# Two score banks held as one lasting tile, and each pair's score products as one chain, in a two-block transformer kernel

## The chip, the cores and the metric

The kernel runs on one core of one Trainium2 chip. The time is that of one execution on the device, in microseconds; the median of three runs stands for the kernel.

The engines of the core work side by side, each through its own queue in order: PE multiplies matrices (its weight loads are shown as PEld), DVE and ACT do vector and activation work, POOL some more vector work, SP starts most transfers. PE writes its products into PSUM, which has banks of 512 float32 columns; DVE and ACT read them from there.

## The reference, cut to what matters

A whole model in float32. The first block has four branches (an attention with forget gates, a gated linear recurrence, a stick-breaking attention, an attention to a memory), a gated merge and a feed-forward part. The second block has two layers, on 256 tokens and 256 context tokens, and in the second layer only the tokens go on. Each layer has three branches, a merge, and 16 experts that choose their tokens:

```python
ka, va, kb, vb, qa, qb, u, v, gates = _split(h @ w_in[i], KV_SIZES + Q_SIZES)
...
ya = neighbourhood_attn(_na_heads(qa), _na_heads(ka), _na_heads(va),
                        _na_heads(kac), _na_heads(vac), na_rpb[i])
kb_all = jnp.concatenate([_da_qk(kbc), rope_2d(_da_qk(kb), tabs)], axis=1)
yb = diff_head_norm(diff_attn_blocks(rope_2d(_da_qk(qb), tabs), kb_all, vb_all, lam),
                    da_subln_g[i], lam_init)
yc = gmlp_gate(jax.nn.gelu(u), jax.nn.gelu(v), gm_ln_g[i], gm_ln_b[i], gm_w_s[i], gm_b_s[i])
x = x + gt1 * branch_merge(ya, yb, yc, gates, w_branch[i], w_out[i])
...
x = x + gt2 * ec_moe(h2, w_router[i], w_e1[i], w_e3[i], w_e2[i])
```

The neighbourhood attention has 8 heads of 64 and adds a bias by position to part of its scores. The differential attention has 4 heads, each with two score matrices of depth 64: it takes the softmax of both and subtracts the second, times a factor lambda, from the first.

## The kernel before, in words

The weights are far too many to stay on the chip. They come from HBM in pieces of 1 MB, started by SP into a ring of buffers. ACT writes the rounded high part of each piece (`wh`, line 88), DVE the remainder (`wl`, line 91), and PE multiplies high by high, low by high and high by low, so that three products stand for one in float32. Operands in the activations are split the same way (`lph`/`lpl`, `hh`/`hl`). These products carry the name `mm` in the trace and are called weight products below. In the expert stage of the second block (`w_e` in the trace) the stream of weights is densest.

Attention is woven into them: `weave` takes so many steps of the weight products of one stage, then one step of an attention that is ready. Layer by layer the neighbourhood attention (`na_attn`) stands beside the projections of the differential attention, and the differential attention (`da_attn`) beside the first merge and the projections of the third branch. An attention's step is a turn of `pipe`, which has three units under way: the output products of unit i-2 (`pv`), the transposes of unit i-1 (`tp`, called turns below; the method is `turn`), and the scores of unit i (`s<-g`). A unit is 128 queries of two heads (neighbourhood) or of one head with its two score matrices (differential). `before` splits the q and k of the next unit into high and low, on ACT and POOL.

The two score matrices of a unit are a pair: `pair()` (line 360) asks a pool for two PSUM buffers with the tag "s", of which the pool has two, and `mm3_pair` (line 364) writes three products into each. As a head is 64 deep, such a product uses 64 of the 128 rows of PE's array, one score matrix the upper 64, the other the lower. Then for each matrix `softmax` follows: the maximum on DVE (line 344, `nm<-s`), the exponential on ACT, which also sums (`g<-s,nm`), the reciprocal on DVE (line 348, `r<-su`). In layer 0 half of the units have 512 columns of scores, half 256; in layer 1 all have 512. That makes 48 units, 32 of 512 columns and 16 of 256.

The same two buffers serve other work, one at a time: the rotary embedding of the differential attention's q and k (`rope`, line 1299, `s<-lb,cst` or `s<-lc,cst` in the trace), the memory attention, the recurrence, the mixing of the third branch, and in the expert stage the router, the gathering of tokens and the scattering of the results (`scatter`, `s<-g,ys`).

The order of the instructions on each engine isn't written out. A scheduler takes the traced program, keeps what depends on what (buffers of a pool included: a tile with the tag "s" may be written when the reader of the tile two before it is done), and sets the order of each engine by priority and by when it expects things to be ready. On the chip each engine then runs its queue in order: an instruction that waits holds up all behind it on its engine.

Of the kernel before, what the change touches and what calls it, by code (L numbers as in the profile page):

```python
# [9 lines left out]
F32 = mybir.dt.float32  # L10
# [65 lines left out]
class K:  # L76
# [276 lines left out]
    def gsplit(self, x):  # L353
# [4 lines left out]
        return h, l  # L358

    def pair(self):  # L360

        return [self.ps.tile([128, 512], F32, tag="s", name="s", bufs=2) for _ in range(2)]

    def mm3_pair(self, outs, abs_):

        for x, y, start, stop in ((0, 0, True, False), (0, 1, False, False), (1, 0, False, True)):
            for out, (a, b) in zip(outs, abs_):
                self.mm(out, a[x], b[y], start, stop)

# [5 lines left out]
    def run(self):  # L375
        nc, tc, a = self.nc, self.tc, self.a
        with ExitStack() as st:
            def pool(name, bufs, **k):
                return st.enter_context(tc.tile_pool(name=name, bufs=bufs, **k))

            self.glob = pool("glob", 1)
            self.small = pool("small", 1)
            self.ring = pool("ring", 3)
            self.ps = pool("ps", 1, space=PSUM)
            self.count = 0
            self.bc = None
            self.sqp = None
            self.pend = []
            self.setup()
            self.fill = self.mods()  # L390
            self.consts = [{}, {}]
            self.every, self.nmod = PLAN["every"], 0
            self.block1()
            self.lper = st.enter_context(tc.tile_pool(name="lper", bufs=1, side="right", reuse_waits="tile"))
            self.hh2, self.hl2 = self.lp("h", [128, KD, 512], F32R), self.lp("l", [128, KD, 512], F32R)
            self.block1_ffn()
            self.every = 0
            for i in range(2):
                self.layer(i)
            self.final()  # L400
# [254 lines left out]
    def fox_attn(self):  # L655
# [5 lines left out]
        def scores(hp):  # L661
            Ps = []

            ss = self.pair()
            for j, s in enumerate(ss):
                r = slice(64 * j, 64 * j + 64)
                self.mm(s[:, 0:128], q[r, hp, 0:128], k[r, hp, 0:128], True, False)
            for j, s in enumerate(ss):
                r = slice(64 * j, 64 * j + 64)
                self.mm(s[:, 128:384], q[r, hp, 128:256], k[r, hp], False, False)  # L670
            for j, s in enumerate(ss):
# [47 lines left out]
    def sb_attn(self):  # L719
# [4 lines left out]
        def weights(hp):  # L724
            Ps = []
            ss = self.pair()
            for j, s in enumerate(ss):
                r = slice(64 * j, 64 * j + 64)
                self.mm(s[:, 0:128], q[r, hp, 0:128], k[r, hp, 0:128], True, False)
            for j, s in enumerate(ss):  # L730
                r = slice(64 * j, 64 * j + 64)
                self.mm(s[:, 128:384], q[r, hp, 128:256], k[r, hp], False, False)
            for s in ss:
# [61 lines left out]
    def lru(self):  # L795
        nc, a = self.nc, self.a
# [29 lines left out]
        for k in range(KD):  # L826
            ps = self.ps.tile([128, 512], F32, tag="s", name="s", bufs=2)
            self.mm(ps[:, 0:256], bd["lru_w_a"][:, k], xc[:, k])
            self.mm(ps[:, 256:512], bd["lru_w_x"][:, k], xc[:, k])
            r = self.gtile()  # L830
# [78 lines left out]
    def mem_attn(self):  # L909
# [5 lines left out]
        def scores(u):  # L915
            h, qb = u
            qs = slice(qb * 128, qb * 128 + 128)
            s = self.ps.tile([128, 512], F32, tag="s", name="s", bufs=2)
            for k in range(2):
                self.mm(s[:, 0:256], mq[:, 2 * h + k, qs], mk[:, 2 * h + k], k == 0, k == 1)  # L920
            P = self.gtile(256)
            self.softmax(s, 256, P)
            return P
# [373 lines left out]
    def rope(self, x):  # L1297
        for m in range(4):
            ps = self.ps.tile([128, 512], F32, tag="s", name="s", bufs=2)[:, :256]
            xm = x[:, m, 0:256]  # L1300
# [95 lines left out]
    def gm_gate(self):  # L1396
# [19 lines left out]
        for t in range(nt):  # L1416
# [3 lines left out]
            self.tt(v, v, lb, ALU.add)  # L1420
            ps = self.ps.tile([128, 512], F32, tag="s", name="s", bufs=2)
            for g in range(4):
# [42 lines left out]
    def moe_pre(self, i):  # L1465
# [26 lines left out]
        self.xs = [self.X, self.XC][:ns]  # L1492
        self.lg = self.ps.tile([128, 512], F32, tag="s", name="s", bufs=2)

# [9 lines left out]
    def moe(self, i, st):  # L1504
# [18 lines left out]
        with tc.tile_pool(name=f"mh{i}", bufs=1, reuse_waits="tile") as hp:  # L1523
# [43 lines left out]
            for t in range(nt):  # L1567
                for kq in range(2):
                    tp = self.ps.tile([128, 512], F32, tag="s", name="s", bufs=2)
                    for k in range(4):  # L1570
# [23 lines left out]
        for e in range(NE):  # L1594
            if e % 4 == 0:
# [7 lines left out]
                for k in range(KD):  # L1603
                    ps = self.ps.tile([128, 512], F32, tag="s", name="s", bufs=2)[:, :ns * 128]
                    for m in range(ns):
# [71 lines left out]
    def scatter(self, i, pi, ys, slot2, aff2, sel, T, xs, gt2):  # L1677
        nc, tmp = self.nc, self.tmp
        sp = self.ps.tile([128, 512], F32, tag="s", name="s", bufs=2)[:, :T]
        self.mm(sp, sel[:, pi], slot2)  # L1680
        ap = self.ps.tile([128, 512], F32, tag="s", name="s", bufs=2)[:, :T]
        self.mm(ap, sel[:, pi], aff2)
# [6 lines left out]
        for ms in ([0], [1]) if ns == 2 and pi == NE // 2 - 1 else [range(ns)]:  # L1689
            if ms == [1]:  # L1690
                self.bc = self.rms_bc([xs[0]], idle=True)
            for d in range(KD):
                ps = self.ps.tile([128, 512], F32, tag="s", name="s", bufs=2)
                t = slice(256 * ms[0], 256 * ms[-1] + 256)
# [110 lines left out]
```

## Time and profile before

| | us |
|---|---|
| runs of the kernel before | 2762.38 median of 3 (2761.77 to 2765.89) |
| the profiled execution | 2762.17 |
| its span, from first to last instruction | 2760.4 |
| PE busy in the span | 2533.3 (92%) |
| DVE busy | 1256.9 (46%) |
| ACT busy | 885.1 (32%) |
| POOL busy | 153.2 (6%) |

The chain of work that ended last puts 81% of the span on PE, 13% on DMA, 4% on DVE and 1% on ACT. The mean granted clock of PE is 0.962 of full speed. Between the span and the execution's time lie 1.8 us.

The busy shares are means over stages that are limited by different things. In a timeline a row is a run of like instructions one after the other on an engine, with the start of the first, the time to the end of the last, and their number; the ends of PE's products are modelled, so neighbouring runs may overlap by a few hundredths of a microsecond. The operands in the shapes of PE's rows are the size of the weights (rows x columns) and the moving operand.

### The profile page before, as it was taken

Reading aid. Unit: us, or ns where it says so; the run is one execution under the profiler, and the core shown is the slowest. Engines: PE = TensorE matmul, PEld = TensorE weight load, DVE = VectorE, ACT = ScalarE, POOL = GpSimd, SP = SyncE. Lnnn points to the kernel's source line nnn. Section 1 sums busy time; section 2 is a strip of 40 time slices with the busy share of each in tenths; the row PEclk is TensorE's granted clock in tenths of the full one; section 3 lists DMA queues with packets and bytes.
Section 4 is the critical chain, followed back from the end, with each engine's and each line's share of the span. In section 5 each row is a group of like instructions: output and inputs, shape, how many; then the busy total and the mean of one; then the engine's idle time right before and its main releaser. Section 6 shows DMA issues by size and latency. Waiting matters only on the chain.

```text
span 2760.4 us, 41216 instructions
## 1 busy us (share of the span) xinstructions
PE 2533.3 (92%) x16928; PEld 1818.5 (66%) x16928; DVE 1256.9 (46%) x2550; ACT 885.1 (32%) x1672; POOL 153.2 (6%) x240
## 2 busy tenths in 40 slices
PE   8999999989999999999999999998999987767676
PEld 8999989979988777788843333335888882212222
DVE  6766675658742556664431221214357761101101
ACT  5754445446442334433220100103334441101011
POOL 1000110000001121100000000001221000000000
PEclk9999999999999999999999999999999998988887
DMA  7454645576674222132799999997443588999997
GB/s 232 156 184 153 199 149 181 174 231 210 201 231 118 68 52 77 53 102 92 264 373 409 409 409 409 409 408 235 102 65 124 185 311 356 409 409 409 409 409 279
DMA packets 361052, 666.15 MB, mean 241 GB/s; under 512 B 14256, under 2 KB 260272, under 8 KB 360864
## 3 DMA queue, kind: packets, MB, share of 16 engines
q1 hardware_dynamic: 354816, 654.15, 65.0%
q0 software_dynamic: 2896, 7.80, 2.4%
q8 instruction: 133, 2.18, 0.3%
q10 hardware_dynamic: 3152, 1.57, 0.2%
q14 instruction: 55, 0.45, 0.0%
HBM read 662.43 MB, written 1.05 MB: 240 GB/s over the span
## 4 chain that ended last, share of the span: by engine, by line
PE 81%; DMA 13%; DVE 4%; ACT 1%; issue 1%; SPq 0%; DVEq 0%; ACTq 0%
PE mm L103 67%; DMA w<-in_w_e 10%; PE s L103 9%; PE pv L103 3%; PE tp L372 3%; DMA lph<-in_w_e 1%; DVE g L100 1%; DMA w<-in_w_ada 1%; DVE X L100 1%; ACT g L88 0%; DMA w<-in_w_in 0%; DVE lpl L100 0%; DVE hT L1661 0%; ACT lph L88 0%; DVE wl L91 0%
## 5 line engine op out<-in xcount | busy, mean ns | idle before, releaser
L91 DVE TENSOR_TENSOR wl<-w,wh 128x1024 fp32r<-128x1024 f32 (+1 forms) x381 | 464.1, 1220 | 387.4 <-ACT wh L88 380.8
L88 ACT ACTIVATE wh<-w 128x1024 fp32r<-128x1024 f32 (+1 forms) x381 | 401.3, 1055 | 565.6 <-PE mm L103 487.5
L103 PE MATMUL mm<-w,xin 128*32 128x512 f32 (+1 forms) x1808 | 389.9, 649 | 68.9 <-DMA w<-in_w_e 67.4
L103 PEld LDWEIGHTS mm<-w,xin 128*32 128x32 f32 (+1 forms) x1808 | 96.2, 126 | 313.0 <-issue 173.4
L100 DVE SCALAR_TENSOR_TENSOR g<-g,mm 128x512 f32<-128x512 f32 (+1 forms) x64 | 43.9, 686 | 566.2 <-ACT g L88 510.6
L103 PE MATMUL mm<-lph,wh 128*128 128x512 f32 (+1 forms) x704 | 251.8, 358 | 2.4 <-DVE la L100 1.3
L103 PE MATMUL mm<-lph,wl 128*128 128x512 f32 (+1 forms) x704 | 248.0, 356 | 0.5 <-DVE wl L91 0.5
L103 PE MATMUL mm<-w,hT 128*32 128x256 f32 (+1 forms) x1320 | 171.7, 531 | 24.9 <-DVE hT L1661 11.2
L88 ACT ACTIVATE g<-mm 128x256 f32<-128x256 f32 (+2 forms) x126 | 57.4, 464 | 377.6 <-PE mm L103 336.3
L88 ACT ACTIVATE ys<-mm 32x256 f32<-32x256 f32 (+1 forms) x96 | 42.9, 447 | 388.7 <-PE mm L103 387.7
L103 PE MATMUL mm<-hh,wh 128*128 128x256 f32 x520 | 150.3, 289 | 2.6 <-ACT wh L88 2.6
L103 PEld LDWEIGHTS mm<-lph,wh 128*128 128x128 f32 x704 | 135.0, 192 | 24.3 <-issue 3.7
L372 PE MATMUL tp<-cst,g 128*128 128x128 f32 (+1 forms) x642 | 105.3, 277 | 48.5 <-DVE g L100 45.6
L103 PEld LDWEIGHTS mm<-lph,wl 128*128 128x128 f32 x704 | 134.4, 191 | 22.8 <-issue 4.5
L103 PE MATMUL mm<-hh,wl 128*128 128x256 f32 x520 | 148.7, 286 | 0.0
L103 PE MATMUL mm<-hl,wh 128*128 128x256 f32 x520 | 148.5, 286 | 0.0
L103 PEld LDWEIGHTS mm<-w,hT 128*32 128x32 f32 (+1 forms) x1320 | 67.2, 139 | 115.4 <-issue 77.6
L103 PE MATMUL mm<-lpl,wh 128*128 128x512 f32 x352 | 140.6, 399 | 0.0
L372 PEld LDWEIGHTS tp<-cst,g 128*128 128x128 f32 (+1 forms) x642 | 72.1, 142 | 97.2 <-issue 44.8
L103 PE MATMUL mm<-la,wh 128*128 128x512 f32 (+1 forms) x512 | 129.2, 340 | 0.1
L103 PE MATMUL mm<-a,wh 128*128 128x256 f32 x640 | 119.3, 286 | 0.0
L100 DVE SCALAR_TENSOR_TENSOR X<-s,mod,X 128x256 f32<-128x256 f32 x96 | 45.4, 483 | 155.2 <-PE s L103 155.2
(354 smaller groups left out, 5276.2 us busy)
## 6 DMA issues: line engine op xcount, KB each, us to landing
w<-in_w_e SPq DMA_DIRECT2D x335, 1024.0 KB, 18.4
w<-in_w_in SPq DMA_DIRECT2D x108, 1024.0 KB, 5.2
lph<-in_w_e SPq DMA_DIRECT2D x49, 1024.0 KB, 18.3
w<-in_w_ada SPq DMA_DIRECT2D x48, 1024.0 KB, 5.4
w<-in_w_up SPq DMA_DIRECT2D x22, 1024.0 KB, 5.2
w<-in_w_branch SPq DMA_DIRECT2D x16, 1024.0 KB, 5.1
w<-in_w_out SPq DMA_DIRECT2D x12, 1024.0 KB, 5.2
w<-in_w_branch SPq DMA_DIRECT2D x24, 512.0 KB, 3.4
```

Source lines behind the costliest of these rows:

```text
L88: return self.nc.scalar.activation(out, in_, func, **k)
L91: return (eng or self.nc.vector).tensor_tensor(out=out, in0=a, in1=b, op=op)
L100: return (eng or self.nc.vector).scalar_tensor_tensor(out=out, in0=a, scalar=s, in1=b, op0=op0, op1=op1)
L103: return self.nc.tensor.matmul(out, lhsT, rhs, start=start, stop=stop)
L372: self.nc.tensor.transpose(out, in_, self.ident[:n, :n])
```

## The change

The pool's two buffers "s" become one PSUM tile of 1024 columns that lasts for the whole program, `s2`, seen as two banks. `pair()` returns both. `sbank()` hands out one of the two, strictly in turn as the program is traced, to all other uses. Since the tile lasts, what may be written when follows from who last read or wrote that bank.

A pair's products run as a chain: in `together()` each product is traced with high priority, and each but the first is held, in PE's order, right behind the one traced before it. The bank that the softmax reads last (bank 1) gets its products first. The order of the three terms changes too: high by low and low by high come first, high by high last, so the first product needs the low part of k, which POOL makes. Operands and results stay the same.

The core of the diff (seven more places replace the pool's tile by `sbank()` as in the last piece; the pair of the stick-breaking attention changes as that of the forget-gate attention does):

```diff
@@ -357,15 +357,40 @@
         self.split(h, l, x, self.nc.gpsimd)
         return h, l
 
+    def sbank(self):
+
+        self.sn ^= 1
+        return self.s2[self.sn]
+
     def pair(self):
 
-        return [self.ps.tile([128, 512], F32, tag="s", name="s", bufs=2) for _ in range(2)]
+        return self.s2
+
+    @contextmanager
+    def together(self):
+
+        mm, last = self.mm, []
+
+        def chained(*a):
+            with self.tc.high_priority():
+                ins = mm(*a)
+            if last:
+                self.tc.keep_in_program_order(ins)
+            last.append(ins)
+            return ins
+
+        self.mm = chained
+        yield
+        del self.mm
 
     def mm3_pair(self, outs, abs_):
 
-        for x, y, start, stop in ((0, 0, True, False), (0, 1, False, False), (1, 0, False, True)):
-            for out, (a, b) in zip(outs, abs_):
-                self.mm(out, a[x], b[y], start, stop)
+
+
+        with self.together():
+            for x, y, start, stop in ((0, 1, True, False), (1, 0, False, False), (0, 0, False, True)):
+                for out, (a, b) in list(zip(outs, abs_))[::-1]:
+                    self.mm(out, a[x], b[y], start, stop)
 
     def transpose(self, out, in_):
         n = in_.shape[0]
@@ -382,6 +407,8 @@
             self.small = pool("small", 1)
             self.ring = pool("ring", 3)
             self.ps = pool("ps", 1, space=PSUM)
+            s2 = self.ps.tile([128, 1024], F32, name="s")
+            self.s2, self.sn = (s2[:, 0:512], s2[:, 512:1024]), 0
             self.count = 0
             self.bc = None
             self.sqp = None
@@ -662,12 +689,13 @@
             Ps = []
 
             ss = self.pair()
-            for j, s in enumerate(ss):
-                r = slice(64 * j, 64 * j + 64)
-                self.mm(s[:, 0:128], q[r, hp, 0:128], k[r, hp, 0:128], True, False)
-            for j, s in enumerate(ss):
-                r = slice(64 * j, 64 * j + 64)
-                self.mm(s[:, 128:384], q[r, hp, 128:256], k[r, hp], False, False)
+            with self.together():
+                for j in (1, 0):
+                    r = slice(64 * j, 64 * j + 64)
+                    self.mm(ss[j][:, 0:128], q[r, hp, 0:128], k[r, hp, 0:128], True, False)
+                for j in (1, 0):
+                    r = slice(64 * j, 64 * j + 64)
+                    self.mm(ss[j][:, 128:384], q[r, hp, 128:256], k[r, hp], False, False)
             for j, s in enumerate(ss):
                 h = 2 * hp + j
                 fh = self.fsel[:, h:h + 1]
...
     def rope(self, x):
         for m in range(4):
-            ps = self.ps.tile([128, 512], F32, tag="s", name="s", bufs=2)[:, :256]
+            ps = self.sbank()[:, :256]
             xm = x[:, m, 0:256]
             self.mm(ps, self.perm, xm)
```

PE's queue around a unit of layer 1's differential attention, before (`mm<-` with `wh`, `wl` or `lph` are weight products, `s<-g` the scores):

```order
L103 MATMUL mm<-wh,lph 128x256
L103 MATMUL s<-g 128x512 x3
L103 MATMUL mm<-wh,lhl 128x256
L103 MATMUL mm<-wl,lph 128x256
L103 MATMUL mm<-wh,lph 128x256
L103 MATMUL s<-g 128x512 x3
L103 MATMUL mm<-wh,lhl 128x256
```

and after:

```order
L103 MATMUL mm<-wl,lph 128x256
L103 MATMUL mm<-lph,wh 128x256
L103 MATMUL s<-g 128x512 x6
L397 MATMUL tp<-cst,g 128x128 x4
L103 MATMUL mm<-lhl,wh 128x256
L103 MATMUL mm<-lph,wl 128x256
```

The two runs of three, one bank each, with three weight products between them, have become one run of six. All 48 units stand so after the change; before, 9 stood as a run of six.

PE's queue at the end of layer 1's differential attention, before (`pv` are output products; the last row is the first weight product of what follows):

```order
L103 MATMUL mm<-lph,wl 128x256
L103 MATMUL s<-g 128x512 x3
L372 MATMUL tp<-cst,g 128x128 x4
L103 MATMUL pv<-lb_18434,g 128x128 x2
L103 MATMUL pv<-lb_18435,g 128x128 x2
L372 MATMUL tp<-cst,g 128x128 x4
L103 MATMUL pv<-lb_18434,g 128x128 x2
L103 MATMUL pv<-lb_18435,g 128x128 x2
L103 MATMUL mm<-lph,wh 128x256
```

and after:

```order
L103 MATMUL mm<-lph,wl 128x256
L103 MATMUL s<-g 128x512 x6
L397 MATMUL tp<-cst,g 128x128 x4
L103 MATMUL pv<-lb_18164,g 128x128 x2
L103 MATMUL pv<-lb_18165,g 128x128 x2
L397 MATMUL tp<-cst,g 128x128 x4
L103 MATMUL s<-g 128x512 x6
L103 MATMUL pv<-lb_18164,g 128x128 x2
L103 MATMUL pv<-lb_18165,g 128x128 x2
L103 MATMUL s<-g 128x512 x6
L397 MATMUL tp<-cst,g 128x128 x4
L103 MATMUL pv<-lb_18164,g 128x128 x2
```

Before, half a pair and then the turns and outputs of two units stand there without weight products. Now three whole pairs do, and the last rows of the piece go on with another output, a turn and two outputs before the weight products return.

PE's queue at the end of layer 0's neighbourhood attention, before (`s<-lb,cst` is a product of the rotary embedding, `s<-g 128x512` at the end the first differential unit):

```order
L103 MATMUL pv<-g,la_10301 64x128 x7
L372 MATMUL tp<-cst,g 128x128 x2
L103 MATMUL s<-g 128x256 x3
L372 MATMUL tp<-cst,g 128x128 x2
L103 MATMUL s<-g 128x256 x3
L103 MATMUL pv<-g,la_10301 64x128 x4
L372 MATMUL tp<-cst,g 128x128 x4
L103 MATMUL pv<-g,la_10301 64x128 x4
L103 MATMUL s<-g 128x512 x2
```

and after, from the first turn behind the last six weight products:

```order
L397 MATMUL tp<-cst,g 128x128 x4
L103 MATMUL s<-lb_10874,cst 128x256
L103 MATMUL pv<-g,la_10254 64x128
L397 MATMUL tp<-cst,g 128x128 x4
L103 MATMUL s<-g 128x512 x6
L103 MATMUL pv<-g,la_10254 64x128 x7
L397 MATMUL tp<-cst,g 128x128 x4
L103 MATMUL s<-lb_10874,cst 128x256
L103 MATMUL pv<-g,la_10254 64x128
L397 MATMUL tp<-cst,g 128x128 x4
L103 MATMUL s<-g 128x256 x6
L103 MATMUL pv<-g,la_10254 64x128 x7
```

Two units of 512 columns and two of 256 now come after the weight products have thinned out (the second of 256 is a few rows further down), where two of 256 came before.

DVE's queue for a unit at the end of layer 1's differential attention, before (`nm<-s` is the maximum, `r<-su` the reciprocal of the sum, `g<-tp` the copy of the transposed scores, `o<-pv` that of the output):

```order
L344 TENSOR_REDUCE nm<-s 128x1
L100 SCALAR_TENSOR_TENSOR g<-g,r 128x512
L344 TENSOR_REDUCE nm<-s 128x1
L91 TENSOR_TENSOR wl<-w,wh 128x1024
L701 COPY g<-tp 128x512
L348 RECIPROCAL r<-su 128x1 x2
L91 TENSOR_TENSOR r<-r,lamv_15012 128x1
L96 TENSOR_SCALAR g<-g,r 128x512
L100 SCALAR_TENSOR_TENSOR g<-g,r 128x512
```

and after:

```order
L344 TENSOR_REDUCE nm<-s 128x1
L729 COPY g<-tp 128x512
L348 RECIPROCAL r<-su 128x1
L344 TENSOR_REDUCE nm<-s 128x1
L348 RECIPROCAL r<-su 128x1
L91 TENSOR_TENSOR r<-r,lamv_14872 128x1
L96 TENSOR_SCALAR g<-g,r 128x512
L1386 COPY o<-pv 128x128
L100 SCALAR_TENSOR_TENSOR g<-g,r 128x512
```

The two maxima came ahead of both reciprocals; now the first bank's reciprocal stands between them, and no `wl` of a weight piece does.

## Rows read from the trace of the kernel before

**Rows 1.** Windows: from, to, length; busy per engine (instructions); clock, DMA share, GB/s.

```profile
860.00:1030.00 170.00, 170.00 (x1015) 133.24 (x1013) 82.30 (x163) 57.01 (x110) 27.61 (x31) 1.00 0.29 70
1030.00:1050.00 20.00, 19.05 (x116) 12.78 (x116) 11.44 (x30) 5.82 (x16) 3.48 (x4) 1.00 0.01 1
...
1137.00:1157.00 20.00, 14.56 (x75) 11.49 (x75) 12.13 (x40) 7.95 (x28) 2.86 (x4) 0.66 0.11 38
...
1385.00:1910.00 525.00, 494.29 (x2334) 192.81 (x2330) 126.99 (x297) 66.04 (x129) 3.78 (x5) 1.00 1.00 391
...
2080.00:2100.00 20.00, 20.00 (x155) 17.64 (x154) 14.18 (x24) 8.82 (x16) 2.60 (x3) 1.00 0.42 128
2100.00:2144.00 44.00, 44.00 (x334) 39.13 (x333) 32.26 (x61) 23.11 (x51) 7.98 (x6) 1.00 0.49 167
2144.00:2160.00 16.00, 11.30 (x66) 9.37 (x65) 13.06 (x35) 6.84 (x19) 2.46 (x4) 0.89 0.60 206
2260.00:2760.00 500.00, 347.03 (x2409) 123.17 (x2408) 62.45 (x150) 55.84 (x131) 0.78 (x2) 0.85 0.96 382
```

**Rows 2.** Groups by shape, layer 0's attentions: count, busy us, mean ns, idle before.

```profile
L103 PE MATMUL s<-g 64*128 64x512 f32 x96 | 23.7, 448 | 0.0
...
L103 PE MATMUL s<-g 64*128 64x256 f32 x96 | 17.1, 347 | 0.0
```

**Rows 3.** The same, layer 1's attentions.

```profile
L103 PE MATMUL s<-g 64*128 64x512 f32 x96 | 25.7, 441 | 0.0
```

**Rows 4.** Timeline of PE, a unit of layer 1: start, us, instruction, count.

```profile
1983.91 0.96 PE L103 MATMUL s<-g 64*128 64x512 f32 x6
```

**Rows 5.** Timeline of PE, another unit of layer 1.

```profile
2047.37 0.97 PE L103 MATMUL s<-g 64*128 64x512 f32 x3
```

**Rows 6.** Timeline of PE, a unit of 256 columns in layer 0.

```profile
929.95 0.62 PE L103 MATMUL s<-g 64*128 64x256 f32 x6
```

**Rows 7.** Timeline of PE, a pair of the forget-gate attention.

```profile
177.23 0.93 PE L103 MATMUL s<-a,a 64*128 64x128 f32 x8
```

**Rows 8.** Timeline of all engines, the end of layer 1's differential attention.

```profile
2146.95 0.96 PE L103 MATMUL s<-g 64*128 64x512 f32 x3
...
2147.95 0.69 DVE L344 TENSOR_REDUCE nm<-s 128x1 f32<-128x512 f32 x1 [0.56 <-PE s L103]
...
2148.74 0.69 ACT L88 ACTIVATE g<-s,nm 128x512 f32<-128x512 f32 x1
2149.33 0.19 ACT L88 ACTIVATION_READ_ACCUMULATOR g<-s,nm 128x1 f32 x1
...
2150.30 0.21 DVE L348 RECIPROCAL r<-su 128x1 f32<-128x1 f32 x2
...
2150.81 0.49 DVE L96 TENSOR_SCALAR g<-g,r 128x512 f32<-128x512 f32 x1
2151.33 0.75 DVE L100 SCALAR_TENSOR_TENSOR g<-g,r 128x512 f32<-128x512 f32 x1
...
2152.23 0.63 PE L372 MATMUL tp<-cst,g 128*128 128x128 f32 x4 [0.64 <-DVE g L100]
...
2152.97 0.69 DVE L701 COPY g<-tp 128x512 f32<-128x512 f32 x1 [0.68 <-PE tp L372]
...
2153.71 1.16 PE L103 MATMUL pv<-lb,g 128*128 128x128 f32 x8 [0.85 <-DVE g L701]
...
2156.15 0.47 PE L103 MATMUL mm<-lph,wh 128*128 128x256 f32 x1 [1.28 <-DVE la L100]
```

**Rows 9.** Timeline of PE, expert stage of layer 0, two units of scattering.

```profile
1474.98 1.98 PE L103 MATMUL s<-g,ys 128*128 128x512 f32 x4
1476.89 2.79 PE L103 MATMUL mm<-w,xin 128*64 128x512 f32 x10
```

**Rows 10.** The same stage, one unit of scattering.

```profile
1713.21 1.12 PE L103 MATMUL s<-g,ys 128*128 128x512 f32 x2
1714.27 1.93 PE L103 MATMUL mm<-w,xin 128*64 128x512 f32 x6
```

More of the change, by code (lines that the diff above doesn't have):

```diff
@@ L1 @@
 import math
-from contextlib import ExitStack
+from contextlib import ExitStack, contextmanager
 import numpy as np
@@ L726, in weights @@
             ss = self.pair()
[L727 to L732, printed above, removed]
+            with self.together():
+                for j in (1, 0):
+                    r = slice(64 * j, 64 * j + 64)
+                    self.mm(ss[j][:, 0:128], q[r, hp, 0:128], k[r, hp, 0:128], True, False)
+                for j in (1, 0):
+                    r = slice(64 * j, 64 * j + 64)
+                    self.mm(ss[j][:, 128:384], q[r, hp, 128:256], k[r, hp], False, False)
             for s in ss:
@@ L826, in lru @@
         for k in range(KD):
-            ps = self.ps.tile([128, 512], F32, tag="s", name="s", bufs=2)
+            ps = self.sbank()
             self.mm(ps[:, 0:256], bd["lru_w_a"][:, k], xc[:, k])
@@ L917, in scores @@
             qs = slice(qb * 128, qb * 128 + 128)
-            s = self.ps.tile([128, 512], F32, tag="s", name="s", bufs=2)
+            s = self.sbank()
             for k in range(2):
@@ L1420, in gm_gate @@
             self.tt(v, v, lb, ALU.add)
-            ps = self.ps.tile([128, 512], F32, tag="s", name="s", bufs=2)
+            ps = self.sbank()
             for g in range(4):
@@ L1492, in moe_pre @@
         self.xs = [self.X, self.XC][:ns]
-        self.lg = self.ps.tile([128, 512], F32, tag="s", name="s", bufs=2)
+        self.lg = self.sbank()
     def moe_front(self, k):
@@ L1568, in moe @@
                 for kq in range(2):
-                    tp = self.ps.tile([128, 512], F32, tag="s", name="s", bufs=2)
+                    tp = self.sbank()
                     for k in range(4):
@@ L1603, in moe @@
                 for k in range(KD):
-                    ps = self.ps.tile([128, 512], F32, tag="s", name="s", bufs=2)[:, :ns * 128]
+                    ps = self.sbank()[:, :ns * 128]
                     for m in range(ns):
@@ L1678, in scatter @@
         nc, tmp = self.nc, self.tmp
-        sp = self.ps.tile([128, 512], F32, tag="s", name="s", bufs=2)[:, :T]
+        sp = self.sbank()[:, :T]
         self.mm(sp, sel[:, pi], slot2)
-        ap = self.ps.tile([128, 512], F32, tag="s", name="s", bufs=2)[:, :T]
+        ap = self.sbank()[:, :T]
         self.mm(ap, sel[:, pi], aff2)
@@ L1692, in scatter @@
             for d in range(KD):
-                ps = self.ps.tile([128, 512], F32, tag="s", name="s", bufs=2)
+                ps = self.sbank()
                 t = slice(256 * ms[0], 256 * ms[-1] + 256)
```

## The prediction

> **What bounds the kernel now.** I read the stretches first, because the mean over the program (PE 92% busy) hides three kinds of stage. In the two attention parts of the second block PE has no gap: 170.00 us busy of 170 between 860 and 1030, 44.00 of 44 between 2100 and 2144, while DVE is busy 82.30 of the 170 us and ACT 57.01 [rows 1]. There a microsecond less on PE is a microsecond less of the span. The first layer's expert stage (1385 to 1910) has PE at 494.29 of 525 us, with its DMA share at 1.00 and the clock full: mostly PE. The second layer's (2260 to 2760) has PE at 347.03 of 500 us under a DMA share of 0.96: it waits for weights. Its transfers run back to back, but start only when the stage before it is done with the buffers, so what is won or lost ahead of it should shift it whole.
>
> Between the full stretches lie the ends of the two attentions, where the weight products beside which they are woven have run out. There PE does wait: 0.95 us of 20 at the end of layer 0's neighbourhood attention (1030 to 1050), 5.44 of 20 at the end of its differential attention (1137 to 1157, clock 0.66), nothing at the end of layer 1's neighbourhood attention (2080 to 2100), 4.70 of 16 at the end of its differential attention (2144 to 2160, clock 0.89) [rows 1]. I call these ends A, B, C and D.
>
> Then the groups of score products, for what they cost altogether, the timeline around single units, for what a pair costs when it runs together, and the timeline of end D, for the latency of one unit without cover.
>
> **The gain: the pairs.** The score products of these two attentions work with 64 rows of the array, so two of them can run side by side if they follow each other. Today they seldom do, since the two banks come free at different times and the scheduler puts weight products between. Altogether they take 23.7 us (512 columns) and 17.1 us (256 columns) in layer 0, and 25.7 us in layer 1 [rows 2, 3]: 66.5 us for 48 units of six products (288 in all). A run of six, both heads in turn, lasts 0.96 us [rows 4]; a run of three, one head alone, 0.97 us [rows 5]. So a whole pair costs what half of one does. With 256 columns a run of six lasts 0.62 us [rows 6]. In the changed order of PE all 48 units are such a run of six: 32 of 512 columns at 0.96 and 16 of 256 at 0.62, 30.7 + 9.9 = 40.6 us. PE gets 66.5 - 40.6 = 25.9 us back; I allow 2 either way, since the modelled ends of neighbouring runs overlap by a few hundredths. The first block's pairs (two banks in one run of eight today [rows 7]) have nothing to win, and I cost that edit at nothing, as I do the new order of the three terms: it needs the low part of k, made by POOL, for the first product, but inside a full stretch POOL is far ahead of it.
>
> What a rule says against this: the Trainium skill (TensorEngine Tiling (Array Packing), PSUM Bottleneck) states that packing quickens TensorE and not the emptying of PSUM, which may then be the bound. Were it so in the whole of both attentions, nothing of the gain would be seen and the time would be that of the losses below alone. By the row of the long stretch, with DVE at half and ACT at a third of the time, it holds only at the ends.
>
> **The losses: the ends.** A pair now needs both banks at once, and its first product is queued on PE behind whatever is placed before it. So a unit cannot start while either bank of the one before is still read by the softmax, and the scheduler's order has moved: more units stand at the ends without weight products beside them. At D three units follow each other with only turns (transposes) and output products between, where one and a half stood. PE being in order, every weight product of the next stage is queued behind them.
>
> What one unit of 512 columns takes there, from the row of each step [rows 8]: scores 0.96, maximum 0.69, exponential 0.69 with its read-out 0.19, reciprocal 0.21, and the same chain for the other bank (0.69, 0.69, 0.19, 0.21), since DVE's changed order puts the first reciprocal ahead of the second maximum; then the factor 0.49, the subtraction 0.75. That is 5.8 us, and about 6.4 with hand-offs of 0.1 between engines (an estimate; today 2146.95 to 2152.23 is 5.28 with both maxima side by side). The second exponential is over about 4.7 us after the start.
>
> *End D.* First chain at 0, its turn at 6.4 (0.63 long). The second chain stands behind that turn: 7.0. The third waits for the second's exponentials: 11.7. DVE finishes the second unit at 13.1 before it takes the third's first maximum; from there 5.4 to the third's turn at 18.5; with turn, copy (0.69) and the output products (1.16) to the next weight product, as today 2152.23 to 2156.15 [rows 8] is 3.9, less 0.7 of DVE's side work: 21.7 us. PE's own work in it is 3 chains (2.9), 4 turns (2.5) and 4 outputs (4.6), 10.0. Idle 11.7 against 4.70: +7.0 (bounds +3 and +9).
>
> *End A.* Two 512 units, each with a bias added to half of the columns of either bank (0.35 each, half of a maximum's price, an estimate). In the steps above, with 0.49 for each scaling and no subtraction, the second turn comes 6.7 us after the chain, the next chain 0.3 later: 14 us for two; then two of 256 columns at some 4.3 and 5.1: 23.4 us. PE's work: chains 3.2, six weight products 2, turns 4, outputs and rope products 6, together 15.2, estimated by the rows of the same kinds. Idle 8 against 0.95: +7 (+3 to +10).
>
> *End B.* Five units of 256 columns, one with eight transposes as cover, for somewhat over three today at half clock. By the same steps at half the columns a unit costs about 4.6 us where nothing covers it; four of them 18 us, with some 9.6 of PE's work, idle 8 against 5.44: +2 (-2 to +5).
>
> *End C.* One 512 unit without cover, where there was none: its outputs come at about 8.5, then two weight products, then the first differential pair, which waits for the split of its k on POOL; 10.5 us with 6.5 of work: +4 (0 to +7).
>
> Together +20. Where PE waits that long the granted clock falls: it stood at 0.66 over end B's 20 us and at 0.89 at D, and at 1.00 at A and C, where PE hardly waited [rows 1]. At A and D some 4 to 5 us of PE's work would be done at the lower level (1.2 GHz) and take twice as long; half of that lies beside DVE's chain anyway. I take +5 (0 to +10).
>
> One more: the lasting pair of banks is dealt out strictly in turn, and this splits products that stood two by two in layer 0's expert stage (12 places, the product that scatters the expert outputs). Two units in a run go from 1474.98 to 1476.89, 1.91 us [rows 9]; one alone from 1713.21 to 1714.27, 1.06 [rows 10]: 0.21 more for two, 12 times, +2.5 (0 to +3). In layer 1's expert stage the DMAs hide it.
>
> The sum: 2762.2 of the profiled execution (0.2 below the median of the three runs), -25.9, +20, +5, +2.5: 2763.8. I forecast 2764: no change that a measurement of this kernel can tell, for which I take 0.2%, 5.5 us either way.
>
> **The rivals.**
> The ends stay short, the gain remains. If the units at the ends start earlier than I have them (in the full stretch the softmax chain gets further ahead than I assume), each loss falls to its lower bound: A +3, C +1, D +4, B 0, clock +2, scatter +2, in all +12: 2762 - 26 + 12 = 2748. For it: DVE has half of its time free in the full stretches. Against it: the order is fixed, and at D a chain stands behind a turn that needs the whole softmax.
>
> The ends are long and the clock falls in each (slower). It is one mechanism: PE starved by the two-bank chain where weight products have run out. Each end at its upper bound short of B (+10, +2, +6, +9), clock +8, scatter +2.5: +37.5 - 25.9 = 2774. It decides from about 32 us of losses. For it: at B, with shorter units, the clock already lies at 0.66. Against it: end A keeps outputs and ropes that fill in.
>
> The pairs gain nothing, since a waiting head product holds its partner: the 25.9 is lost in new waits inside the full stretches. Then 2762 + 27.5, some 2790. Against it: the runs of six that stand there today cost 0.96 [rows 4], and 20 or more weight products lie between units.
>
> **How the numbers follow.** The forecast case has 0.40 (2756 to 2769, nearly all of it within 0.2%), short ends 0.28, long ends 0.27, no gain from pairs 0.05. Faster by over 0.2%: 0.28; within: 0.37; slower: 0.35, which takes in the long ends, the lost gain and a sliver of the forecast case. The range, 2748 to 2779, leaves out the lower half of the short ends and the case without gain.
>
> **What would show it.** In the profile after: score runs of six, all at 0.96 or 0.62, summing to about 41 us; PE busy down by 20 or more and its idle up by as much; at the four ends, gaps of 8, 8, 4 and 12 us with DVE's reciprocal, maximum and exponential ended last, and the clock below 0.8 at A and D. The second expert stage as long as now, only shifted. I am wrong if the ends' idle time sums to under 22 us (today 11) or over 45, or if a chain inside a full stretch waits for ACT.

## The result: 89 us slower, and the profile after

The changed kernel takes 2851.34 us (median of 4 runs, 2847.11 to 2854.57) against 2762.48 before: ratio 1.0318, 95% interval 1.03 to 1.0336. I had said 2764, with a range to 2779. The profiled execution took 2850.76 us, 88.6 more than that of before.

The page of the profile after, first the busy time and then the span in 40 slices (tenths of busy time, tenths of the granted clock, busy share of the DMA engines):

```profile
PE 2563.0 (90%) x16928; PEld 1831.4 (64%) x16928; DVE 1266.3 (44%) x2550; ACT 888.6 (31%) x1672; POOL 146.8 (5%) x240
...
PE   8999999989999989899998989898999897767675
...
PEclk9999999999999999899998989898999898788887
DMA  7455555576663312225898989896443488999996
```

PE's busy time did not fall by 20 us as I expected, but rose by 30 (2533.3 before). The clock and the DMA share have holes where the expert stage of layer 0 stands (slices 20 to 27): the weight stream, which ran without a pause there, stops and starts.

The stretches that answer to [rows 1], in the same columns: the full stretch of layer 0, the ends A and B, the expert stage, the full stretch of layer 1, the ends C and D, the second expert stage.

```profile
860.00:1010.00 150.00, 150.00 (x948) 123.81 (x946) 69.19 (x131) 52.19 (x96) 24.41 (x27) 1.00 0.34 79
1010.00:1050.00 40.00, 29.43 (x182) 18.74 (x181) 24.90 (x62) 10.84 (x29) 7.36 (x8) 0.91 0.00 1
...
1126.00:1164.00 38.00, 24.92 (x142) 19.57 (x141) 26.90 (x83) 14.89 (x52) 4.32 (x6) 0.66 0.09 28
1385.00:1983.00 598.00, 543.92 (x2438) 209.65 (x2436) 134.31 (x332) 70.43 (x145) 4.59 (x8) 0.93 0.90 348
2032.00:2140.00 108.00, 108.00 (x815) 97.79 (x813) 52.76 (x85) 39.92 (x68) 19.38 (x22) 1.00 0.42 96
2140.00:2160.00 20.00, 16.70 (x113) 12.01 (x111) 14.60 (x30) 6.48 (x14) 2.86 (x4) 0.89 0.26 80
...
2208.00:2240.00 32.00, 20.36 (x109) 16.33 (x108) 21.05 (x48) 11.72 (x33) 4.34 (x6) 0.70 0.42 147
2330.00:2848.00 518.00, 358.65 (x2506) 138.34 (x2504) 69.10 (x160) 59.63 (x137) 0.78 (x2) 0.83 0.95 378
```

The full stretches are still full. At the ends PE idles 10.6, 13.1, 3.3 and 11.6 us, 38.6 in all (11.1 before). The expert stage of layer 0 takes some 590 us (8 of the window belong to the stage before) for what took 525.

The score products, layer 0 (two rows) and, over a window of layer 1, 90 of its 96 (the first unit lies ahead of it), to hold against [rows 2, 3]:

```profile
L103 PE MATMUL s<-g 64*128 64x512 f32 x96 | 16.1, 442 | 0.0
...
L103 PE MATMUL s<-g 64*128 64x256 f32 x96 | 11.5, 351 | 1.4 <-ACT g L88 1.4
```

```profile
L103 PE MATMUL s<-g 64*128 64x512 f32 x90 | 15.2, 444 | 1.6 <-ACT g L88 1.6
```

16.1 + 11.5 + 15.2 x 96/90 = 43.8 us against 66.5: the pairs do run side by side, and PE gets 22.7 us back.

To see where the time goes, I set the traces side by side at the same piece of weights, counted from the start by DVE's rows `wl`. The table gives how far each kernel is behind the one before (us, less is ahead). Two of the experiments below stand beside the change.

| piece starts, before | what lies up to it | changed kernel | two tiles (e1) | scattering moved (e5) |
|---|---|---|---|---|
| 1010 | first block, full stretch of layer 0 | -18.3 | -15.0 | -19.6 |
| 1053 | end A | +1.4 | -10.2 | +0.1 |
| 1128 | differential attention, layer 0 | -9.5 | -18.7 | -10.8 |
| 1190 | end B | +8.4 | -11.4 | +7.1 |
| 1922 | expert stage, layer 0 | +73.8 | -11.2 | +4.6 |
| 2078 | full stretch of layer 1 | +60.1 | -14.7 | -9.1 |
| 2096 | end C | +72.9 | -16.3 | +3.7 |
| 2144 | differential attention, layer 1 | +65.1 | -20.9 | -4.0 |
| 2168 | end D | +81.4 | -16.1 | +12.2 |
| end | expert stage, layer 1 | +88.6 | -16.3 | +12.3 |

The first block shows nothing (-0.4 us at the piece that starts at 800). The attentions cost 8.4 us in layer 0 and 6.4 in layer 1 (+75.0 at the piece that starts at 1970, before the first of them, to +81.4); the expert stage of layer 0 costs 65.4, that of layer 1 another 7.2. The 1.2 us that are left lie between 1922 and 1970.

What happens in layer 0's expert stage is in the timeline of one place where eight scattering products follow each other (start, duration, instruction, in brackets the idle time before and what ended it):

```profile
1531.88 1.12 PE L103 MATMUL s<-g,ys 128*128 128x512 f32 x2 [0.68 <-ACT ys L88]
1533.04 0.48 DVE L100 SCALAR_TENSOR_TENSOR X<-s,mod,X 128x256 f32<-128x256 f32 x1 [8.37 <-PE s L103]
1533.44 0.48 DVE L100 SCALAR_TENSOR_TENSOR lpl<-s,mod,lpl 128x256 f32<-128x256 f32 x1
...
1533.97 1.65 PE L103 MATMUL s<-g,ys 128*128 128x512 f32 x2 [0.97 <-DVE lpl L100]
1535.66 0.48 DVE L100 SCALAR_TENSOR_TENSOR X<-s,mod,X 128x256 f32<-128x256 f32 x1 [1.74 <-PE s L103]
1536.07 0.47 DVE L100 SCALAR_TENSOR_TENSOR lpl<-s,mod,lpl 128x256 f32<-128x256 f32 x1
...
1536.59 2.07 PE L103 MATMUL s<-g,ys 128*128 128x512 f32 x2 [0.97 <-DVE lpl L100]
...
1554.93 2.07 PE L103 MATMUL s<-OH,xt 128*128 128x128 f32 x8 [0.97 <-DVE lpl L100]
```

Each product writes the other bank than the one before it, and yet starts only when DVE has read the one before: PE multiplies, DVE reads, PE multiplies. PE falls to the lower level of its clock meanwhile (granted 0.72 between 1530 and 1540, 0.50 between 1540 and 1560), as the durations show too (1.12, then 2.07), and the period becomes 3.05 us. The last row is the next other work, a gathering product. The same place before:

```profile
1516.95 1.98 PE L103 MATMUL s<-g,ys 128*128 128x512 f32 x4 [0.68 <-ACT ys L88]
1519.14 1.96 PE L103 MATMUL s<-g,ys 128*128 128x512 f32 x4 [0.20 <-DVE lpl L100]
1521.30 1.96 PE L103 MATMUL s<-g,ys 128*128 128x512 f32 x4 [0.20 <-DVE lpl L100]
...
1525.62 0.57 PE L103 MATMUL s<-OH,xt 128*128 128x128 f32 x3 [0.20 <-DVE lpl L100]
```

There two products (four records) go together and the wait is 0.20: 1.08 us for each. The stage has three such places, eight products in a row in PE's order before and after alike. Each took 8.66 us before, from its first product to the next other one; after, they take 23.05, 20.63 and 23.21: 40.9 of the 65.4 us. The scattering products of the stage in one row, after and before (busy us, mean ns, idle before):

```profile
L103 PE MATMUL s<-g,ys 128*128 128x512 f32 x112 | 79.3, 797 | 24.8 <-DVE lpl L100 22.8 <-ACT ys L88 2.1
```

```profile
L103 PE MATMUL s<-g,ys 128*128 128x512 f32 x112 | 56.3, 619 | 3.9 <-ACT ys L88 2.0 <-DVE lpl L100 1.8
```

So the waits weigh about as much as the longer products, which now run singly and in part at the lower clock: 20.9 us more of idle time, 23.0 more of busy time. PE's waits in the whole stage (waiting for, us in total, times, longest), after and before:

```profile
PE s L103 <- DVE lpl L100: 28.5, 33, 1.1
```

```profile
PE s L103 <- DVE lpl L100: 2.4, 12, 0.2
```

After, 24 of the 33 last 0.97 us or a little more, the others 0.5 to 0.6.

The ends tell the same. End D after, DVE and ACT beside PE:

```profile
2221.07 1.65 PE L103 MATMUL s<-g 64*128 64x512 f32 x6
...
2222.76 0.69 DVE L344 TENSOR_REDUCE nm<-s 128x1 f32<-128x512 f32 x1 [0.89 <-PE s L103]
2223.49 0.69 ACT L88 ACTIVATE g<-s,nm 128x512 f32<-128x512 f32 x1 [5.53 <-DVE nm L344]
...
2224.30 0.16 DVE L348 RECIPROCAL r<-su 128x1 f32<-128x1 f32 x1 [0.84 <-ACT g L88]
2224.38 0.67 DVE L344 TENSOR_REDUCE nm<-s 128x1 f32<-128x512 f32 x1
...
2225.14 0.69 ACT L88 ACTIVATE g<-s,nm 128x512 f32<-128x512 f32 x1 [0.88 <-DVE nm L344]
...
2225.97 0.97 PE L103 MATMUL s<-g 64*128 64x512 f32 x6 [1.57 <-ACT g L88]
```

The second maximum reads a bank that was written at the same time as the first, but comes only after the first bank's exponential. After the change this is so in all 48 units; before, the two maxima stand side by side in DVE's order in 43, and with two tiles (e1 below) in all 48.

### The profile page after: what moved, and what is told of

The parts are those of the page before. It is cut to its first block, busy times and chain, and to the rows that moved or that the text cites. A ratio compares the mean times of both kernels' runs of the same rounds, so it can differ in the third digit from the quotient of the medians.

```text
span 2849.0 us, 41231 instructions
## 1 busy us (share of the span) xinstructions
PE 2563.0 (90%) x16928; PEld 1831.4 (64%) x16928; DVE 1266.3 (44%) x2550; ACT 888.6 (31%) x1672; POOL 146.8 (5%) x240
## 4 chain that ended last, share of the span: by engine, by line
PE 47%; DMA 10%; DVE 5%; issue 1%; ACT 1%; SPq 0%; DVEq 0%; ACTq 0%
PE mm L103 35%; PE s L103 8%; DMA w<-in_w_e 7%; DMA lph<-in_w_e 2%; PE pv L103 2%; DVE X L100 1%; PE tp L397 1%; DVE g L100 1%; DMA w<-in_w_ada 1%; DVE lpl L100 1%; SPq L1618 0%; ACT g L88 0%; DVE nm L344 0%; DVE hT L1690 0%; DVE g L96 0%
## 5 line engine op out<-in xcount | busy, mean ns | idle before, releaser
L103 PE MATMUL mm<-w,hT 128*32 128x256 f32 (+1 forms) x1320 | 169.7, 513 | 24.8 <-DVE hT L1690 10.4
L103 PE MATMUL s<-g,ys 128*128 128x512 f32 (+1 forms) x208 | 122.2, 677 | 47.5 <-DVE lpl L100 24.5
L103 PEld LDWEIGHTS mm<-lph,wl 128*128 128x128 f32 x704 | 135.0, 192 | 19.6 <-issue 1.1
## 6 DMA issues: line engine op xcount, KB each, us to landing
lph<-in_w_e SPq DMA_DIRECT2D x49, 1024.0 KB, 18.3
```

What stands on the lines that cost most here:

```text
L103: return self.nc.tensor.matmul(out, lhsT, rhs, start=start, stop=stop)
```

## The experiments

My theory after the result, theory 1 below: whatever touches one half of the lasting tile is put in order with whatever touches the other half, in the program's order, reads with reads too (the maximum behind the exponential). The tile, not the chain, does the harm. The rivals: the chain, which needs both banks at once; the strict turn of `sbank`. Besides the pairs, ten places take a bank from `sbank` (nine beside that of `rope`, not seven as I wrote). All ratios are against the kernel before on the same chip. The experiments ran on two chips, and their 95% intervals reach some 3 to 5 us to either side, so the order of two experiments that lie closer than that is open.

**e1, two lasting tiles.**

```diff
-            s2 = self.ps.tile([128, 1024], F32, name="s")
-            self.s2, self.sn = (s2[:, 0:512], s2[:, 512:1024]), 0
+            self.s2, self.sn = [self.ps.tile([128, 512], F32, name=f"s{j}") for j in range(2)], 0
```

> The changed kernel with one edit: the two banks are two lasting tiles of 512 columns instead of two halves of one. Chain, order of terms and strict turn-taking stay. Theory 1, that whatever touches one half of the one tile is ordered against whatever touched the other half: the score pairs still run six in a row, the scattering products of layer 0's expert stage run two by two again, each unit's two maxima stand side by side again; 2735 to 2760 us. Rival, the chain that needs both banks at once: only the scattering is mended, the ends of the attentions stay as long, 2775 to 2795. Second rival, the strict turn-taking: no change, 2845 or more.

2745.76 us, ratio 0.9939 (0.9925 to 0.9954). Theory 1 holds and both rivals fall: the one line is worth some 105 us, and with it the rest of the change is a gain. The same eight scattering products, and then the ends A, B, C, D and the expert stage between (the windows are shifted with the work):

```profile
1506.98 4.08 PE L103 MATMUL s<-g,ys 128*128 128x512 f32 x8 [0.68 <-ACT ys L88]
1511.27 1.95 PE L103 MATMUL s<-g,ys 128*128 128x512 f32 x4 [0.20 <-DVE lpl L100]
```

```profile
995.00:1045.00 50.00, 46.19 (x271) 32.49 (x270) 32.39 (x73) 16.14 (x39) 7.55 (x8) 1.00 0.13 43
1105.00:1150.00 45.00, 36.76 (x257) 32.18 (x256) 31.07 (x91) 18.43 (x60) 5.34 (x8) 0.81 0.11 35
1375.00:1915.00 540.00, 508.07 (x2439) 206.90 (x2438) 139.64 (x325) 75.51 (x149) 7.56 (x9) 0.99 0.99 386
2060.00:2085.00 25.00, 25.00 (x206) 22.97 (x202) 18.83 (x35) 13.08 (x26) 4.34 (x5) 1.00 0.39 121
2115.00:2150.00 35.00, 29.71 (x197) 26.65 (x197) 28.32 (x73) 16.84 (x40) 4.20 (x6) 0.80 0.49 166
```

The scattering runs on without the wait, and PE's idle time at the ends is 3.8, 8.2, 0 and 5.3, 17.3 us against 38.6.

**e2, the pool's two tiles with the chain.** `sbank()` asks the pool for a tile with the tag "s" again, `pair()` for two.

> The changed kernel with the pool's two tiles of before in place of the lasting tile; the chain and the new order of terms and banks stay. Theory 1 (the one tile does the harm): 2735 to 2765 us, like two lasting tiles. Rival (the chain does the harm): 2775 or more.

2757.33 us, 0.9985 (0.9976 to 0.9995). Within what theory 1 said, far from the chain rival, but 12 us behind e1. In PE's order 22 of 48 pairs stand as one and five, as the pool gives out its two tiles one by one. The profiled run also loses 8 us in the first block; but it is itself 5 us slower than the median (2762.28 us), and whether the others lose them there is not shown.

**e3, one lasting tile without the chain.**

```diff
-            with self.tc.high_priority():
-                ins = mm(*a)
-            if last:
-                self.tc.keep_in_program_order(ins)
-            last.append(ins)
-            return ins
+            return mm(*a)
```

> The changed kernel with the one lasting tile, but without the chain: the pair's products are traced at plain priority and not held behind each other (the order of terms and banks stays). Theory 1: as slow as the changed kernel, 2830 to 2865 us, nearly all score runs still six long because the one tile serves them together. Rival (the chain): back to 2755 to 2775.

2862.64 us, 1.0363 (1.0348 to 1.0379). The tile is as slow without the chain, even 11 us slower.

**e5, the scattering out of the tile.** In `scatter`, `ps = self.sbank()` becomes a pool tile with the tag "tp".

> The changed kernel, but the products that scatter the expert outputs go to the two tiles of the transposes instead of the one lasting tile; the attentions keep it. Theory 1 puts some 68 of the 89 us into layer 0's expert stage, where each of these products waits for the reading of the one before it: 2780 to 2800 us. Rival (the expert stage is late because the stages before it end late, or for its transfers): above 2835.

2775.37 us, 1.0047 (1.0032 to 1.0062): 76.0 us come back, a little more than the 68 I had put there. In the table, the stage costs nothing now (+7.1 to +4.6) and layer 1's expert stage is free of its 7.2 too.

**e6, two tiles, but the scattering all in one of them.** `ps = self.s2[0]` in `scatter`.

> Two lasting tiles as in e1 (2745.8 us), but all products that scatter the expert outputs go to the first of them, so that each has to wait for the reading of the one before it, and nothing else is touched. Theory: this alone is the loss of layer 0's expert stage, 50 to 80 us on top: 2796 to 2826 us, with about 1 us of idle PE before each such product and lower granted clock where eight follow each other. Rival (the expert stage suffers from something else of the one tile, such as the router or the gathering): below 2770.

2796.89 us, 1.0138 (1.0121 to 1.0155): 51.1 us on top of e1. The serial products by themselves make a loss of that kind, at the low end of what I expected; against the kernel before, layer 0's expert stage gets 41 us longer, not the 65 of the change, and layer 1's 9.

**e11, the gathering in the same bank.** As e6, with the gathering and the two products that prepare a scattering also in the first tile. The second of these two overwrites the first before it is read, so the scattering of this kernel adds wrong rows; the work is the same.

> As e6 (2796.9 us: two lasting tiles, the scattering products all in the first), and the products that gather an expert group's tokens, and the two that prepare a scattering, go to the first tile as well. In the changed kernel the expert stage of layer 0 took some 66 us more than before, in e6 only some 41. Theory: the rest comes from the gathering products, which one tile ties to the scattering as well: 2812 to 2830 us. Rival (the gathering has cover enough): 2792 to 2802.

2820.30 us, 1.0224 (1.0206 to 1.0242), and the stage is 65 us longer: the missing part comes from the other products of the stage that share the tile, the gathering and the two that prepare, which this run does not tell apart.

**e10, the rotary embedding out of the tile too.** As e5, and `rope` takes a tile with the tag "tp".

> The changed kernel with both the scattering products and those of the rotary embedding in the two tiles of the transposes (e5 moved the scattering alone: 2775.4 us). The pairs keep the one lasting tile, and DVE still has each unit's second maximum behind the first bank's exponential. Theory: the 30 us by which e5 stays behind two lasting tiles (2745.8) are the pairs' own serial softmax at the ends, so 2768 to 2778 us. Rival (they come from the rotary embedding that shares the tile with the pairs): 2745 to 2760.

2754.06 us, 0.998 (0.9971 to 0.999). The rival was right: about 20 of the 30 us between e5 and e1 come from the rotary embedding in the same tile as the pairs. Some 8 to 11 are left for the serial softmax and whatever else shares the tile, which no run separates. The trace places this: PE idles 3.5 us at end A (46.47 busy of 50 us), 10.6 in the changed kernel, but 13.1 at end B as there (24.93 of 38). In the changed kernel a rotary product waits until the later of a unit's two exponentials is over, with the pair of the next unit behind it in PE's order (end A):

```profile
1024.01 0.70 PE L103 MATMUL s<-lb,cst 128*128 128x256 f32 x2 [0.75 <-ACT g L88]
...
1025.59 0.96 PE L103 MATMUL s<-g 64*128 64x512 f32 x6
```

**What the parts of the good version are worth.** e7 is e1 without the chain (the edit of e3), e8 is e1 with the order of terms and banks of before, e4 is the kernel before with the new order of terms and banks alone, e9 is e1 with a quicker pace of weaving (`+ 3` to `+ 6`, `+ 4` to `+ 8`).

> Two lasting tiles as in e1, but the pair's products are traced at plain priority and not held together. 24 of 48 units are still one run of six in PE's order, the others mostly three and three. Theory (the pairs running side by side are the gain, 22 us of PE's time in e1): about half of it is lost, 2752 to 2760 us. Rival (the gain comes from the lasting tiles and the new order of terms): 2743 to 2749.

2758.46 us, 0.9992 (0.9983 to 1.0001). The theory holds: the chain is worth 12.7 us of e1's gain. On PE it is worth more: the score products take 62.9 us here and 43.2 in e1 (44.6 + 18.3 against 32.1 + 11.1 for the two widths).

> Two lasting tiles and the chain as in e1, with the order of terms and banks of before (high by high first, first bank first). In PE's order most units stand as one and five or two and four, since the first bank comes free before the second and its products are started early. Theory: each split costs 0.2 to 0.4 us of PE, 2750 to 2758 us. Rival (the order of banks doesn't matter): 2743 to 2748.

2751.58 us, 0.9968 (0.9957 to 0.998): as the theory had it, the bank read last must be written first, or the chain's first products start on the other bank and the pair falls apart (38 of 48). Worth 5.8 us.

> The kernel before (the pool's two tiles, no chain), with the new order of terms and banks alone. In PE's order 26 of 48 units now stand as one run of six, against 9 before. Theory (runs of six are what gains): 2752 to 2760 us. Rival (the order of terms is neutral without the chain): 2760 to 2765.

2755.73 us, 0.9986 (0.9977 to 0.9996): that order alone lets 26 pairs run together in the pool's tiles, for some 4 us (1 to 6 by the interval).

> Two lasting tiles as in e1, and the attentions are woven in at a quicker pace (the number of steps that the weaving counts with is raised from 8 or 16 plus 3 to plus 6 for the neighbourhood attention, and from plus 4 to plus 8 for the differential one), so that fewer units are left when the weight products run out. Theory (what is left of the loss is at the ends): 2735 to 2744 us. Rival (a quicker pace makes PE wait inside the stretches, as the softmax can't follow): 2748 or more.

2748.52 us, 0.9956 (0.9944 to 0.9969). The theory falls. The time is at the edge of the rival's range, 2.8 us behind e1, with overlapping intervals; but the rival's mechanism is not in the trace, where PE is busy without a gap inside the stretches (140.00 of 140 us from 860 to 1000, 80.00 of 80 from 1975 to 2055). The ends idle no less than in e1: 3.5, 10.4, 0 and 5.8 us, 19.7 in all. Why the quicker pace does not shorten them stays open.

## Why the prediction was wrong

**The step that failed** is the last of the losses: "this splits products that stood two by two in layer 0's expert stage (12 places, the product that scatters the expert outputs) ... +2.5 (0 to +3)". I saw in the order of PE that pairs of scattering products had become single ones, and priced the split by the start of a run, from [rows 9, 10]. I didn't ask why the scheduler had split them. It had because the second had to wait for the reading of the first. Where nothing covers it, one costs not 0.1 us but a wait of 0.97, and where eight follow each other the lower clock as well. Most of the loss is not in the 12 places at all: the three runs of eight, +40.9 us, look the same in the order before and after, and I gave them no price. That stage lives from an unbroken weight stream (DMA share 1.00 in [rows 1], 0.90 after), and the time does not come back: 65.4 us for +2.5. The upper bound, +3, came from the same reading and so was no bound. Behind it stands a sentence from ahead of the prediction, that what may be written when follows from who last read or wrote "that bank": in these runs it follows from who last touched the tile.

Of the 87 us between the forecast and the profiled run, the scattering is 63; the attentions are 16 (+14.8 measured for -25.9 + 20 + 5 = -0.9), layer 1's expert stage 7, and 1 lies between the stages.

**The cause of the ends.** I wrote that "a pair now needs both banks at once", and that this starves PE where the weight products have run out. The price at the ends was near: 38.6 us of idle PE measured, 8 + 8 + 4 + 11.7 = 31.7 predicted, D 11.6 against 11.7. That is luck in part, since the mechanism was another. The order of DVE, with the first reciprocal ahead of the second maximum, was in the reckoning, but I took it as the scheduler's choice and did not ask for its reason. The cause was for the most part not the chain: e1 keeps it, and its ends idle 17.3 us. Of the 6 us that this is above the 11.1 of before, some 4 go with the chain, as the ends of e7, without it, idle 13.2. Had I asked what makes DVE wait with a maximum whose operand is ready, I might have found the tile, and with it the expert stage.

**The clock at the ends** was put at +5, with less than 0.8 expected at A and D. It stood at 0.91, 0.66, 0.89 and 0.70 (A to D): D as I said, A not, and B at the 0.66 of before but over a window of 38 us instead of 20. The attentions' balance, 8.4 + 6.4 = 14.8 us, is the pairs' -22.7 and the additional idle time of 27.5, which leaves 10. If that is the clock, it is twice my term; no run shows it by itself.

**The gain** was mis-sized by little: 22.7 us of PE's time for a predicted 25.9 ("I allow 2 either way"), because runs took 1.00 and 0.72 us on the mean (16.1 and 11.5 us for 16 units each), not the 0.96 and 0.62 of [rows 4, 6]; some of each stood at the lower clock at the ends (1.65 us at D above). With two tiles the chain gives back 19.7 us of PE's time (62.9 in e7, 43.2 in e1) and 12.7 of the kernel's; some 4 of the difference are the idle time at the ends.

**Layer 1's expert stage** I had hidden behind the DMAs, at nothing; it lost 7.2 us. The scattering products wait there too: 19.6 us in 32 places for DVE's reading, 2.9 in 12 before; e5, which takes them out of the tile, gives the 7.2 back.

**The bounds.** The rivals did not add up the bounds as stated: all lower bounds make +4 instead of +12 (about 2740 us), all upper ones short of B +41 instead of +37.5 (about 2777). Neither comes near the result.

**Right** were the first block, which shows nothing; the order of the terms, whose wait for POOL appears in no full stretch; and all 48 runs of six. The rule of the Trainium skill (TensorEngine Tiling (Array Packing), PSUM Bottleneck) was weighed rightly for the full stretches, which stay full (150.00 of 150 us). At the ends PE does wait for the reading, but most of what the change added goes with the order of the two halves, which e1 lifts (38.6 us of idle time against 17.3), and so does the wait in the expert stage, whose products use all 128 rows.

## What to carry to other kernels

If two banks are to be written and read independently, give each its own tile: here two halves of one tile were ordered like one, and the line that joins them cost some 105 us. When an order shows that instructions which stood together have come apart, or that an engine takes a ready operand late, look for the dependency behind it before pricing it, and take a split for a wait until the opposite is shown. Then look for the same dependency where the order has not changed: the three costliest places looked the same before and after. And price a wait by its stage: in one that lives from an unbroken stream of transfers, as here, it is not made up later.

The fastest version here is e1, 2745.76 us: two lasting tiles, the chain, the bank read last written first.

## What the runs showed that I had not expected

In the expert stage the weight stream does not make up what PE loses. Its DMA share was 1.00 before, at 391 GB/s on the mean [rows 1]; during the eight serial scattering products shown above it came nearly to a stop, some 18 us after the first of them (windows of the changed kernel, columns as before):

```profile
1540.00:1550.00 10.00, 7.00 (x8) 1.64 (x7) 2.63 (x6) 0.00 (x0) 0.00 (x0) 0.50 1.03 408
1550.00:1560.00 10.00, 7.07 (x20) 4.07 (x18) 2.16 (x5) 0.46 (x1) 0.00 (x0) 0.50 0.09 37
```

PE at half of its clock, with DVE busy for a quarter of the time, held up a stream that had no reserve: in the windows from 1600 to 1680, between this stop and the next, its share is 1.02 to 1.03, as it was before the stop and in the kernel before, and no more. The queue that starts these transfers waits for PE for up to 28.2 us at a time in this stage, 5.7 before.
